# Attention in pairs of row groups: one value bank, narrower side windows and three copies a unit

## The chip, the cores and the metric

One core of a Trainium2 chip runs the whole program. The metric is the device time of one execution in microseconds; lower is better. TensorE (PE) does matrix products and transposes, VectorE (DVE) and ScalarE (ACT) elementwise work, GpSimd (POOL) some adds and a few DMAs, and SyncE's queue (SP) issues nearly all DMAs.

## What is computed

A backbone of two layers over 1024 latent tokens (a grid of 16 rows and 64 columns) and 256 context tokens, width 1024, float32. Each layer normalises and modulates, projects into three groups (a bidirectional mLSTM, a neighbourhood attention, a gated linear recurrence), projects the joined results back and adds an MLP. The change lies in the attention alone. Cut to what matters of it:

```python
for each latent query (row r, column c), 8 heads of 64 channels:
    keys  = 8 rows x 16 columns of the grid around it, and all 256 context tokens
    s     = q . k / 8 (+ relative-position bias on the grid keys)
    o     = softmax(s) @ v
context queries (first layer only): softmax(q . k_ctx / 8) @ v_ctx
```

## The kernel before

Two heads go together (`hp`, 0 to 3); `e` is the head in the pair. `na_prep` loads q and k of two heads, normalises them, transposes them and splits them into two float32r parts (`KH`, `KL`, and `QS` with both parts of q one above the other), so that a score is the sum of two products. `na_att(hp, ...)` is then the attention of these two heads. It runs for 4 pairs of heads in 2 layers.

A unit is one query tile of 128 queries for both heads. In the first layer the context gives two units (256 queries). The latents give eight: four column tiles `b` of 16 query columns, each with two row groups `g` of 8 query rows. A latent unit does, in this order:
- scores (L795, L799): keys of 12 grid rows (11 for `g` = 0) by 32 columns beginning at column 0, 8, 24 or 32, so 384 or 352 columns of one PSUM bank a head, and 256 context keys of both heads in a third bank. Each is two products (`KH`, `KL`). They take all three banks of tag "a".
- softmax: for each head VectorE adds the table (bias and masks, `tab`, 32 columns a key row) and takes the minimum of the negated scores (L809), then the same over the context keys (L813); ScalarE's exponential (L816) writes `S` and the sums `den`.
- `side()`: steps of other work, which are the preparation of the next two heads and half of the output projection (L1325, evacuated by VectorE at L1342 to the residual in DRAM).
- `softmax_pv`: ten transposes of `S` on TensorE (L688), five key tiles for each head: four tiles of head 0 into one bank, four of head 1 into another, the last context tile of both into a third (tags "b", "b", "q", which take turns and are also used by `na_prep`). They are copied into `PT`: head 0's by ScalarE (L705), head 1's by VectorE (L707), the third bank by ScalarE (L690). In row group 0 the third key tile has 96 keys only, so its two banks need three copies each, since tiles of one height go together.
- the sums: a reciprocal of `den` (L710), a copy that spreads it over 64 channels a head (L712, `rb`), and its transpose (L714) into the one bank of tag "c".
- the value products (L718) into the same bank, 64 channels of either head side by side: values `VB` of the grid (four tiles of 4 rows x 32 columns, loaded by four DMAs at L778, three buffers) and `VC` of the context.
- the exit (L826, L827; L755, L756 for the context): ScalarE copies the result into `yr`, VectorE multiplies it by the transposed reciprocals, which it reads in the bank.

A planner of the framework orders the instructions of each engine when the program is built: it takes, of those that it thinks ready by its own durations, the one that was traced first, and adds all semaphore waits. So an engine's order can differ from the traced one, but once built it is fixed, and a waiting instruction holds all behind it. A tile's buffer comes free when its last reader is done. `bank(tag)` gives a PSUM bank; the numbers of banks are p 1, q 1, a 3, b 2, c 1.

## Time and profile before

| | |
|---|---|
| median of 3 runs | 3128.67 us (3122.56 to 3129.33) |
| span of the profiled execution | 3122.6 us |
| TensorE busy | 3016.5 us (97%) |
| VectorE busy | 1898.7 us (61%) |
| ScalarE busy | 1129.1 us (36%) |
| first attention stretch | 528 to 735 us |
| second attention stretch | 2140 to 2348 us |

Busy time is the time in which an engine had at least one instruction under way. Matmuls overlap in the engine, so a row's duration is longer than what the instruction holds the engine for; the distance between two starts tells that. The granted clock (PEclk) is a share of full speed.

### The profile page before, as it was taken

Reading aid. Unit: us, or ns where it says so; the run is one execution under the profiler, and the core shown is the slowest. Engines: PE = TensorE matmul, PEld = TensorE weight load, DVE = VectorE, ACT = ScalarE, POOL = GpSimd, SP = SyncE. Lnnn points to the kernel's source line nnn. Section 1 sums busy time; section 2 is a strip of 40 time slices with the busy share of each in tenths; the row PEclk is TensorE's granted clock in tenths of the full one; section 3 lists DMA queues with packets and bytes.
Section 4 is the critical chain, followed back from the end, with each engine's and each line's share of the span. In section 5 each row is a group of like instructions: output and inputs, shape, how many; then the busy total and the mean of one; then the engine's idle time right before and its main releaser. Section 6 shows DMA issues by size and latency. Waiting matters only on the chain.

```text
span 3122.6 us, 47473 instructions
## 1 busy us (share of the span) xinstructions
PE 3016.5 (97%) x18250; PEld 2553.0 (82%) x18250; DVE 1898.7 (61%) x4318; ACT 1129.1 (36%) x2011; POOL 288.9 (9%) x252
## 2 busy tenths in 40 slices
PE   7999998999899999999999999998899999999999
PEld 6888887878788888887778889997787777887877
DVE  5757654887887666455444584755787444444444
ACT  4632223674422222233222453234564223332222
POOL 0410010122200000010000511002222000000000
PEclk9999999999899999999999999999999999999999
DMA  9624667865233444233333532348753332343333
GB/s 272 223 73 124 174 172 206 234 186 176 67 109 109 123 127 124 79 108 99 92 94 95 176 122 82 101 123 222 223 169 113 95 95 88 99 117 90 93 96 93
DMA packets 531098, 410.73 MB, mean 132 GB/s; under 512 B 27580, under 2 KB 496536, under 8 KB 530872
## 3 DMA queue, kind: packets, MB, share of 16 engines
q1 hardware_dynamic: 519448, 387.41, 42.1%
q0 software_dynamic: 8576, 15.00, 1.5%
q10 hardware_dynamic: 2848, 5.28, 0.6%
q8 instruction: 144, 2.36, 0.3%
q14 instruction: 82, 0.67, 0.1%
HBM read 339.72 MB, written 67.53 MB: 130 GB/s over the span
## 4 chain that ended last, share of the span: by engine, by line
PE 70%; DVE 11%; DMA 10%; issue 2%; ACT 2%; SPq 1%; POOL 0%; ACTq 0%; DVEq 0%; POOLq 0%
PE psa L436 15%; PE psa L1477 14%; PE psq L436 5%; PE psp L436 5%; PE psp L1477 5%; PE psq L1477 5%; PE psp L451 4%; DMA mr<-in_w_mod_dram 4%; PE psq L451 4%; PE psp L1325 2%; DVE ma L312 2%; PE psc L718 2%; DVE wl L201 1%; PE psa L1325 1%; PE psb L688 1%
## 5 line engine op out<-in xcount | busy, mean ns | idle before, releaser
L200 ACT ACTIVATE wh<-wr 128x1024 fp32r<-128x1024 f32 (+3 forms) x356 | 361.6, 1021 | 946.5 <-PE psa L1477 307.3
L201 DVE TENSOR_TENSOR wl<-wr,wh 128x1024 fp32r<-128x1024 f32 (+3 forms) x356 | 425.0, 1198 | 386.4 <-ACT wh L200 380.0
L436 PE MATMUL psa<-xlo,wh 128*128 128x512 f32 (+1 forms) x856 | 319.7, 374 | 2.2 <-DVE xlo L412 2.2
L436 PE MATMUL psa<-xh,wh 128*128 128x512 f32 (+1 forms) x856 | 319.4, 373 | 2.4 <-ACT xh L411 2.3
L436 PE MATMUL psa<-xh,wl 128*128 128x512 f32 (+1 forms) x856 | 319.6, 373 | 1.4 <-DVE wl L201 1.4
L1477 PE MATMUL psa<-hl,wh 128*128 128x512 f32 (+1 forms) x768 | 286.0, 373 | 0.6 <-DVE hl L211 0.6
L1477 PE MATMUL psa<-hh,wh 128*128 128x512 f32 (+1 forms) x768 | 284.2, 375 | 0.3 <-ACT wh L200 0.3
L1477 PE MATMUL psa<-hh,wl 128*128 128x512 f32 (+1 forms) x768 | 277.9, 373 | 0.6 <-DVE wl L201 0.6
L1481 DVE SCALAR_TENSOR_TENSOR res<-psa,modt,res 128x512 f32<-128x512 f32 (+1 forms) x192 | 131.0, 693 | 170.3 <-PE psa L1477 169.9
L436 PEld LDWEIGHTS psa<-xh,wh 128*128 128x128 f32 x856 | 162.1, 190 | 33.4 <-ACT xh L411 3.1
L436 PEld LDWEIGHTS psa<-xlo,wh 128*128 128x128 f32 x856 | 162.1, 189 | 33.1 <-DVE xlo L412 2.6
L436 PEld LDWEIGHTS psa<-xh,wl 128*128 128x128 f32 x856 | 162.1, 189 | 32.3 <-DVE wl L201 2.2
L377 POOL TENSOR_TENSOR acc<-acc,nsq 128x512 f32<-128x512 f32 (+1 forms) x56 | 77.9, 1401 | 1026.9 <-ACT nsq L376 976.5
L1477 PEld LDWEIGHTS psa<-hh,wh 128*128 128x128 f32 x768 | 144.3, 188 | 34.6 <-ACT wh L200 8.6
L451 PE MATMUL psp<-wl,xh 128*128 128x256 f32 (+1 forms) x560 | 164.0, 293 | 4.3 <-DVE wl L201 4.2
L1477 PEld LDWEIGHTS psa<-hh,wl 128*128 128x128 f32 x768 | 144.3, 188 | 28.7 <-DVE wl L201 1.5
L1477 PEld LDWEIGHTS psa<-hl,wh 128*128 128x128 f32 x768 | 144.4, 188 | 27.4 <-DVE hl L211 0.8
L210 ACT ACTIVATE hh<-rl 128x512 fp32r<-128x512 f32 (+1 forms) x160 | 93.5, 589 | 202.1 <-DVE rl L1453 202.0
L451 PE MATMUL psp<-wh,xh 128*128 128x256 f32 (+1 forms) x560 | 161.9, 289 | 2.4 <-ACT wh L200 2.4
L451 PE MATMUL psq<-wh,xh 128*128 128x256 f32 (+1 forms) x560 | 161.7, 289 | 1.4 <-ACT usq L605 0.9
L451 PE MATMUL psq<-wl,xh 128*128 128x256 f32 (+1 forms) x560 | 160.6, 287 | 0.0
L451 PE MATMUL psp<-wh,xlo 128*128 128x256 f32 (+1 forms) x560 | 159.9, 286 | 0.0
(409 smaller groups left out, 7328.5 us busy)
## 6 DMA issues: line engine op xcount, KB each, us to landing
wr<-in_w_mlp_dram SPq DMA_DIRECT2D x256, 512.0 KB
mr<-in_w_mod_dram SPq DMA_DIRECT2D x92, 512.0 KB
wr<-in_w_in_dram SPq DMA_DIRECT2D x48, 512.0 KB
tab<-T_d SPq DMA_DIRECT2D x48, 384.0 KB
T_d<-E_d POOLq DMA_DIRECT2D x48, 256.0 KB, 6.6
ab<-row_d SPq DMA_DIRECT2D x36, 256.0 KB
xT_d<-res SPq DMA_DIRECT2D x4, 2048.0 KB
wr<-in_w_out_dram SPq DMA_DIRECT2D x32, 256.0 KB
```

What stands on the lines that cost most here:

```text
L200: act.activation(hi[:, a:b], raw[:, a:b], AF.Copy)
L201: dve.tensor_sub(lo[:, a:b], raw[:, a:b], hi[:, a:b].bitcast(F32))
L210: act.activation(hi, src32, AF.Copy)
L312: dve.scalar_tensor_tensor(a, raw[:, k], s[:, k], a, op0=OP.mult, op1=OP.add)
L377: pool.tensor_add(acc[bi], acc[bi], sq[:, :n])
L436: m = pe.matmul(t[:, :n], w[a][:, k, :], X[bi][b][:, k, :], start=(i == 0), stop=(i == 23))
L451: pe.matmul(t[:, :cols], X[bi][b][:, half * 4 + k, o:o + P], ws[half][a][:, k, :], start=(i == 0), stop=(i == 23))
L688: pe.transpose(t[:w, j * P:(j + 1) * P], S[e][:, o:o + w], permT)
L718: pe.matmul(to[64 * e:64 * e + 64, :P], vals[i][:w, 64 * e:64 * e + 64], PT[:w, e, i], start=(i == 0), stop=(i == nt - 1))
L1325: pe.matmul(t[:, :n], w[a][:, k, cc * P:(cc + 1) * P], Y[bi][b][:, k], start=(i == 0), stop=(i == 11))
L1477: m = pe.matmul(t[:, :n], w[a][:, k, cc * P:(cc + 1) * P], H[bi, k][b], start=(i == 0), stop=(i == 3 * GH - 1))
L1481: dve.scalar_tensor_tensor(xr[bi][:, ct], t[:, :n], G2[:, ct, v:v + 1], xr[bi][:, ct], op0=OP.mult, op1=OP.add)
```

## The change

`softmax_pv` is split. `transposed` does the ten transposes and their copies: with the new layout all grid tiles of a unit have one height `w`, and three banks with four, two and four tiles get one copy each (VectorE, ScalarE, ScalarE). `pv` does the sums and the value products of both units of a pair, with the products in the first half of one bank "c" and the transposed reciprocals in the second, and one exit for 256 queries. The reciprocal is taken of the spread sums directly. A pair is the two row groups of a column tile, or the two context tiles. The outer column tiles (`b` = 0 and 3) take 24 key columns (from 0 and from 40), the inner ones 32; every unit takes 12 key rows. `PT` has three buffers instead of two, `VB` two instead of three. The rest of the difference removes comments and is left out here.

```diff
-        def softmax_pv(npl, S, den, tiles, vals, permT, ydst):
-            PT = npl.tile([P, 2, 5, P], F32, name=nm("PT"), tag="PT", bufs=2)
-            nt = len(tiles)
-            if nt == 2:
-                groups = [[(0, 0), (0, 1), (1, 0), (1, 1)]]
-            else:
-                groups = [[(0, i) for i in range(4)], [(1, i) for i in range(4)], [(0, 4), (1, 4)]]
-            for gi, gr in enumerate(groups):
+        def transposed(npl, S, w, permT):
+            PT = npl.tile([P, 10, P], F32, name=nm("PT"), tag="PT", bufs=3)
+            tl = [(e, i * w, w) for e in range(2) for i in range(3)] if w else []
+            tl += [(e, 3 * w + i * P, P) for e in range(2) for i in range(2)]
+            o = 10 - len(tl)
+            for a, b, q in ((0, 4, dve), (4, 6, act), (6, 10, act)):
+                if a < o:
+                    continue
                 t = bank("bbq")
-                for j, (e, i) in enumerate(gr):
-                    o, w = tiles[i]
-                    pe.transpose(t[:w, j * P:(j + 1) * P], S[e][:, o:o + w], permT)
-                if len(gr) == 2:
-                    act.activation(PT[:, :, 4], t[:, 0:2 * P].rearrange("p (k q) -> p k q", q=P), AF.Copy)
-                    continue
-                if nt == 2:
-                    act.activation(PT[:, :, 0:2], t.rearrange("p (e k q) -> p e k q", e=2, q=P), AF.Copy)
-                    continue
-                e = gi
-                j = 0
-                while j < 4:
-                    j2 = j
-                    w = tiles[j][1]
-                    while j2 < 4 and tiles[j2][1] == w:
-                        j2 += 1
-                    src = t[:w, j * P:j2 * P].rearrange("p (k q) -> p k q", q=P)
-                    if e == 0:
-                        act.activation(PT[:w, e, j:j2], src, AF.Copy)
-                    else:
-                        dve.tensor_copy(PT[:w, e, j:j2], src)
-                    j = j2
-            dve.reciprocal(den, den)
-            rb_ = npl.tile([P, 2, 64], F32, name=nm("rb"), tag="rb", bufs=2)
-            dve.tensor_copy(rb_, den.unsqueeze(2).to_broadcast([P, 2, 64]))
+                h = tl[a - o][2]
+                for j in range(a, b):
+                    e, c, _ = tl[j - o]
+                    pe.transpose(t[:h, (j - a) * P:(j - a + 1) * P], S[e][:, c:c + h], permT)
+                src = t[:h, 0:(b - a) * P].rearrange("p (k q) -> p k q", q=P)
+                if q is dve:
+                    dve.tensor_copy(PT[:h, a:b], src)
+                else:
+                    act.activation(PT[:h, a:b], src, AF.Copy)
+            return PT
+        def pv(npl, units, permT, ydst):
             to = bank("c")
-            pe.transpose(to[:, P:2 * P], rb_.rearrange("p e d -> p (e d)"), permT)
-            for i in range(nt):
-                w = tiles[i][1]
-                for e in range(2):
-                    pe.matmul(to[64 * e:64 * e + 64, :P], vals[i][:w, 64 * e:64 * e + 64], PT[:w, e, i],
-                              start=(i == 0), stop=(i == nt - 1))
-            ydst(to[:, :P], to[:, P:2 * P])
+            for u, (PT, den, loc, w, vc) in enumerate(units):
+                rb_ = npl.tile([P, 2, 64], F32, name=nm("rb"), tag="rb", bufs=2)
+                dve.reciprocal(rb_, den.unsqueeze(2).to_broadcast([P, 2, 64]))
+                pe.transpose(to[:, (2 + u) * P:(3 + u) * P], rb_.rearrange("p e d -> p (e d)"), permT)
+            for u, (PT, den, loc, w, vc) in enumerate(units):
+                n = len(loc) + 2
+                for i in range(n):
+                    for e in range(2):
+                        es = slice(64 * e, 64 * e + 64)
+                        if i < len(loc):
+                            v, p_ = loc[i][:w, es], PT[:w, 3 * e + i]
+                        else:
+                            c = i - len(loc)
+                            v, p_ = vc[:, c, es], PT[:, 6 + 2 * e + c]
+                        pe.matmul(to[es, u * P:(u + 1) * P], v, p_, start=(i == 0), stop=(i == n - 1))
+            ydst(to[:, 0:2 * P], to[:, 2 * P:4 * P])
 
         anchors = []
 
         def new_den():
             return sm.tile([P, 2], F32, name=nm("den"), tag="den", bufs=4)
         def na_att(hp, npl, stacks, yr, side):
             QS, KH, KL = stacks
             VC = npl.tile([P, 2, P], F32, name=nm("VC"), tag="VC", bufs=1)
             uv = u_nv[l]
             sp.dma_start(VC, uv[0:NCTX, hp * P:(hp + 1) * P].rearrange("(t p) c -> p t c", p=P))
             if not last:
+                units = []
                 for qt in range(2):
                     tS = bank("a")
                     S = []
...
                         dve.tensor_scalar(nmx, mx, -1.0, None, op0=OP.mult)
                         act.activation(s_[:, :256], sv, AF.Exp, bias=nmx, accum_out=den[:, e:e + 1])
                         S.append(s_)
-                    def yd(t, r, qt=qt):
-                        act.activation(yr[:, qt * P:(qt + 1) * P], t, AF.Copy)
-                        dve.tensor_mul(yr[:, qt * P:(qt + 1) * P], yr[:, qt * P:(qt + 1) * P], r)
                     side()
                     phase(f"na_att{l}")
-                    softmax_pv(npl, S, den, [(0, P), (P, P)], [VC[:, 0], VC[:, 1]], ident, yd)
+                    units.append((transposed(npl, S, 0, ident), den, [], 0, VC))
+                def yd(t, r):
+                    act.activation(yr[:, 0:2 * P], t, AF.Copy)
+                    dve.tensor_mul(yr[:, 0:2 * P], yr[:, 0:2 * P], r)
+                pv(npl, units, ident, yd)
             for ct, bs in enumerate(((0,), (1, 2), (3,))):
                 tab = []
                 for e in range(2):
...
                     pool.tensor_add(tv, tv, crm[ct].rearrange("p (r c) -> p r c", c=32))
                     tab.append(tb_)
                 for b in bs:
-                    VB = npl.tile([P, 4, P], F32, name=nm("VB"), tag="VB", bufs=3)
-                    c0 = (0, 8, 24, 32)[b]
+                    cw = (24, 32, 32, 24)[b]
+                    kc = (0, 8, 24, 40)[b]
+                    to = 8 if b == 3 else 0
+                    w = 4 * cw
+                    nl = 3 * w
+                    VB = npl.tile([P, 4, P], F32, name=nm("VB"), tag="VB", bufs=2)
                     for r in range(4):
-                        sp.dma_start(VB[r * 32:(r + 1) * 32],
+                        sp.dma_start(VB[r * cw:(r + 1) * cw],
                                      bass.AP(tensor=uv.tensor,
-                                             offset=uv.offset + (NCTX + r * 64 + c0) * 512 + hp * P,
-                                             ap=[[512, 32], [4 * 64 * 512, 4], [1, P]]))
+                                             offset=uv.offset + (NCTX + r * 64 + kc) * 512 + hp * P,
+                                             ap=[[512, cw], [4 * 64 * 512, 4], [1, P]]))
+                    units = []
                     for g in range(2):
-                        nr = 11 if g == 0 else 12
-                        nl = nr * 32
-                        r0 = 0 if g == 0 else 4
-                        kc = (0, 8, 24, 32)[b]
+                        r0 = 4 * g
                         qo = NCTX + (1 - g) * 512 + (3 - b) * P
                         tC = bank("a")
                         tL = []
...
                             tl = bank("a")
                             tL.append(tl)
                             for i, K_ in enumerate((KH, KL)):
-                                kv = K_[e][:, NCTX:].rearrange("p (r c) -> p r c", c=64)[:, r0:r0 + nr, kc:kc + 32]
-                                pe.matmul(tl[:, :nl].rearrange("p (r c) -> p r c", c=32), QS[e][:, qo:qo + P], kv,
+                                kv = K_[e][:, NCTX:].rearrange("p (r c) -> p r c", c=64)[:, r0:r0 + 12, kc:kc + cw]
+                                pe.matmul(tl[:, :nl].rearrange("p (r c) -> p r c", c=cw), QS[e][:, qo:qo + P], kv,
                                           start=(i == 0), stop=(i == 1))
                         for e in range(2):
                             for i, K_ in enumerate((KH, KL)):
...
                         S = []
                         den = new_den()
                         for e in range(2):
                             s_ = npl.tile([P, 640], F32, name=nm("S"), tag="S", bufs=4)
                             m1_ = sm.tile([P, 1], F32, name=nm("m1"), tag="m1", bufs=4)
                             m2_ = sm.tile([P, 1], F32, name=nm("m2"), tag="m2", bufs=4)
-                            dve.tensor_tensor_reduce(out=s_[:, 0:nl], in0=tL[e][:, :nl],
-                                                     in1=tab[e][:, 1 - g, 0:nl],
-                                                     scale=-1.0, scalar=3.0e38, op0=OP.add, op1=OP.min,
+                            tv = tab[e][:, 1 - g].rearrange("p (r c) -> p r c", c=32)[:, :, to:to + cw]
+                            dve.tensor_tensor_reduce(out=s_[:, 0:nl].rearrange("p (r c) -> p r c", c=cw),
+                                                     in0=tL[e][:, :nl].rearrange("p (r c) -> p r c", c=cw),
+                                                     in1=tv, scale=-1.0, scalar=3.0e38, op0=OP.add, op1=OP.min,
                                                      accum_out=m1_)
                             dve.tensor_tensor_reduce(out=s_[:, nl:nl + 256], in0=tC[:, e * 256:(e + 1) * 256],
                                                      in1=zcol.to_broadcast([P, 256]), scale=-1.0, scalar=m1_,
...
                             act.activation(s_[:, :nl + 256], s_[:, :nl + 256], AF.Exp, bias=m2_, scale=-1.0,
                                            accum_out=den[:, e:e + 1])
                             S.append(s_)
-                        tiles = [(i * P, min(P, nl - i * P)) for i in range(3)] + [(nl, P), (nl + P, P)]
-                        vals = [VB[:, i + g] for i in range(3)] + [VC[:, 0], VC[:, 1]]
-                        def yd(t, r, b=b, g=g):
-                            cs = slice(16 * b, 16 * b + 16)
-                            tv = t.rearrange("p (r c) -> p r c", r=8)
-                            dst = yr[:, NCTX:].rearrange("p (r c) -> p r c", c=64)[:, 8 * g:8 * g + 8, cs]
-                            act.activation(dst, tv, AF.Copy)
-                            dve.tensor_mul(dst, dst, r.rearrange("p (r c) -> p r c", r=8))
                         side()
                         phase(f"na_att{l}")
-                        softmax_pv(npl, S, den, tiles, vals, flip, yd)
+                        units.append((transposed(npl, S, w, flip), den, [VB[:, i + g] for i in range(3)], w, VC))
+                    def yd(t, r, b=b):
+                        dst = yr[:, NCTX:].rearrange("p (r c) -> p r c", c=64)[:, :, 16 * b:16 * b + 16]
+                        act.activation(dst, t.rearrange("p (r c) -> p r c", r=16), AF.Copy)
+                        dve.tensor_mul(dst, dst, r.rearrange("p (r c) -> p r c", r=16))
+                    pv(npl, units, flip, yd)
```

## Rows read from the trace of the kernel before

**Rows 1.** page, busy us of each engine (share of the span) and instructions
```profile
PE 3016.5 (97%) x18250; PEld 2553.0 (82%) x18250; DVE 1898.7 (61%) x4318; ACT 1129.1 (36%) x2011; POOL 288.9 (9%) x252
```

**Rows 2.** windows: stretch, length, busy us by engine, granted clock, DMA
```profile
528.00:735.00 207.00, 196.41 (x1603) 166.82 (x1604) 166.73 (x551) 132.54 (x344) 43.31 (x24) 0.98 0.69 197
630.00:680.00 50.00, 46.38 (x410) 38.83 (x408) 44.63 (x152) 37.54 (x98) 11.67 (x6) 0.97 0.69 192
2140.00:2348.00 208.00, 191.75 (x1521) 157.58 (x1520) 157.38 (x498) 121.80 (x307) 47.21 (x25) 0.97 0.75 213
```

**Rows 3.** waits of PE, 528 to 735 us: total, times, longest
```profile
PE psc L714 <- DVE yr L827: 2.4, 3, 1.1
PE psb L688 <- ACT S L816: 0.9, 1, 0.9
```

**Rows 4.** waits of PE, 2140 to 2348 us
```profile
PE psa L795 <- DVE m L809: 3.9, 4, 2.3
PE psa L799 <- DVE m L813: 3.1, 3, 2.3
```

**Rows 5.** timeline of PE, score products: start, us, what
```profile
646.35 0.28 PE L741 MATMUL psa<-KL,QS 128*128 128x256 f32 x1
646.47 0.33 PE L795 MATMUL psa<-KH,QS 128*128 128x352 f32 x1
646.63 0.33 PE L795 MATMUL psa<-KL,QS 128*128 128x352 f32 x1
...
653.71 0.34 PE L795 MATMUL psa<-KL,QS 128*128 128x384 f32 x1
653.89 0.28 PE L799 MATMUL psa<-KH,QS 128*128 128x256 f32 x1
```

**Rows 6.** timeline of PE, value products of one unit
```profile
640.42 0.27 PE L688 MATMUL psb<-idj,S 128*128 128x128 f32 x1
640.53 0.27 PE L714 MATMUL psc<-idj,rb 128*128 128x128 f32 x1
640.74 0.88 PE L718 MATMUL psc<-PT,VB 128*64 128x128 f32 x12
641.44 0.61 PE L718 MATMUL psc<-PT,VC 128*64 128x128 f32 x8
641.98 0.66 PE L688 MATMUL psb<-idj,S 128*128 128x128 f32 x4
```

**Rows 7.** line L714, what ended its engine's idle time: us, times
```profile
  DVE yr L827: 6.7, 10
  DVE rb L712: 2.5, 1
```

**Rows 8.** lines by shape, DVE, 528:735: count, busy us, mean ns, idle
```profile
L809 DVE CUSTOM_DVE_ANT_0 S<-psa,tab 128x384 f32<-128x384 f32 x32 | 17.1, 550 | 2.8 <-PE psa L795 2.7
L809 DVE CUSTOM_DVE_ANT_0 S<-psa,tab 128x352 f32<-128x352 f32 x32 | 16.0, 515 | 0.9 <-PE psb L688 0.5 <-issue 0.4
L827 DVE TENSOR_TENSOR yr<-yr,psc 128x128 f32<-128x128 f32 x28 | 7.8, 278 | 0.8 <-ACT yr L826 0.7
L707 DVE COPY PT<-psb 128x512 f32<-128x512 f32 x11 | 7.6, 688 | 2.4 <-PE psb L688 1.7 <-PE psc L718 0.7
L707 DVE COPY PT<-psb 128x256 f32<-128x256 f32 x11 | 4.6, 422 | 2.1 <-PE psc L718 2.1
```

**Rows 9.** lines by shape, DVE, whole span
```profile
L712 DVE COPY rb<-den 128x128 f32<-128x128 f32 x72 | 26.3, 365 | 4.8 <-PE psc L714 3.3
L710 DVE RECIPROCAL den<-den 128x2 f32<-128x2 f32 x72 | 11.4, 159 | 9.0 <-ACT S L816 7.2 <-ACT S L751 1.5
L1248 DVE RECIPROCAL rc<-dn 128x4 f32<-128x4 f32 x36 | 6.2, 175 | 0.7
L1247 DVE TENSOR_TENSOR dn<-dn,tmg 128x4 f32<-128x4 f32 x36 | 5.8, 162 | 0.8
```

**Rows 10.** waits of the SP queue, 528 to 735 us
```profile
SPq L778 <- PE psc L718: 5.9, 8, 1.4
```

## The prediction, made before the changed kernel was run

> **What bounds the kernel now.** I read the page first: TensorE is busy for 97% of the span, VectorE for 61% [rows 1]. The edit touches only the attention, so I looked for the two stretches in which its lines run and cut them out: 528 to 735 us in the first layer, 2140 to 2348 us in the second [rows 2]. There TensorE is busy for 196.4 of 207 and 191.8 of 208 us, VectorE for 166.7 and 157.4, ScalarE for 132.5 and 121.8. So TensorE is the bound with some 27 us of open gaps, and VectorE is the next one. A look inside the first stretch shows how near: in 630 to 680 us VectorE is busy for 44.6 of 50 us, and TensorE misses 3.6. The granted clock was 0.98 and 0.97 over the two stretches, so short spells at the lower level cost some 4 and 6 us there [rows 2].
>
> Then the waits: in the first layer TensorE's longest named wait is the transpose of the reciprocal sums (L714), which waits for the product into yr (L827) to leave the single bank "c"; in the second it is the scores, waiting for VectorE to read the three "a" banks [rows 3, 4]. Both point to VectorE as the one that TensorE waits for. The span (3122.6 us) is that of the lowest of the three runs (3122.56), so nothing to speak of lies around it; I work in differences and set them against the median, 3128.67.
>
> **The change, part by part.** There are 72 units (a unit: one query tile of two heads): 64 of latents, 8 of context in the first layer; in pairs, 36.
>
> Score columns. TensorE's price is not the duration of a row but the distance from one start to the next: 0.16 us for 352 columns, 0.18 for 384, 0.12 for 256 [rows 5]. That is (0.18 - 0.12) / 128 = 0.47 ns a column, and 0.135 us for the new 288. A side tile has four such products in either row group: 4 x (0.16 - 0.135) + 4 x (0.18 - 0.135) = 0.28 us less. A middle tile goes from 352 to 384 in one group: 4 x 0.02 = 0.08 more. There are 16 pairs of each: 16 x (0.08 - 0.28) = **-3.2 us** on TensorE, in work that nothing hides, since TensorE is the bound.
>
> Value products. They are 64 columns wide, two side by side. Going in costs something: the transpose of the sums takes 0.21 us to the next start where a transpose among its like takes 0.11. Going out too: twelve products take 0.70 us, so eight should take 0.47, and the last eight take 0.54 [rows 6]. That is 0.10 + 0.07 a unit. If both units' products stand together, 36 of 72 such passages go: 36 x 0.17 = **-6.1 us**. Bounds: -6.1, or 0 if the planner lets the first unit's products go ahead alone.
>
> One bank and one exit a pair. TensorE waited ten times for yr at L714, 6.7 us counted on its weight loads [rows 7]. The bank changes hands half as often and with another unit's work between; I take **-2 us**, with 0 and -6.7 as bounds, since part of a wait that goes is taken over by the next one.
>
> Three copies a unit. ScalarE and VectorE do the copies, and neither is the bound. For the first row group VectorE's copies of 256, 128 and 128 columns (0.42, and twice 0.28, as its product of that size) become one of 512, 0.69 [rows 8]: 0.29 x 32 units = 9.3 us less VectorE work. But the first bank now holds three tiles of the first head and one of the second, so its copy can't start before the second head's exponential; before, it needed the first head's alone. In the first stretch TensorE's transposes waited 0.9 us in all for exponentials [rows 3]; a share like that again gives **+1 us**; bounds 0 and ten times that.
>
> Side tables and exit on VectorE. The table sum took 0.550 us for 384 columns and 0.515 for 352 [rows 8], 1.1 ns a column. Side tiles save 64 and 96 columns in each of two heads, 16 pairs: 5.6 us; middle tiles give back 1.1. Two yr products of 0.278 us [rows 8] become one of 256 columns, about 0.42 as the copy of that size: 0.14 x 36 = 5 us.
>
> Reciprocals. Before: a reciprocal of two elements (0.159 us) and a copy that spreads it over 128 (0.365 on average). Now: one reciprocal over all 128 [rows 9]. No row shows one of that size. From below, a VectorE operation of 128 columns takes 0.28 us [rows 8]. From above: the reciprocals of 2 and of 4 elements take 159 and 175 ns, while a plain product of 4 elements takes 162 [rows 9]. So two more elements cost 16 ns, 8 ns each, and 128 would take 0.159 + 126 x 0.008 = 1.17 us. I take the upper end, because its rows are of the same operation. That is 1.17 - 0.52 = 0.65 us more a unit, 72 x 0.65 = 47 us. [...]
>
> So VectorE gains 47 - 9.3 - 4.5 - 5 = 28 us of work over both stretches: 324 becomes 352 of 415 us, 85%. It is not the bound on average. What is exposed is the latency before L714: its matmul needs the reciprocal of the second unit, and behind the waiting transpose stand the next pair's scores on TensorE. Of 72 such transposes 11 found VectorE late [rows 7], a share of 0.15. With 0.65 us more in each of 36 pairs, 36 x 0.65 x 0.15 = **+3.5 us**. Bounds: below nothing, -2, if the reciprocal is as short as the lower price, and 36 x 1.3 = +47 if both reciprocals of every pair are waited for.
>
> Buffers. The value tile VB has two buffers instead of three, and each of its four loads, which stand in SP's one queue, waits for the products two tiles back; behind them stand weights, tables and the rows of the side work. With three buffers the queue waited 5.9 us for this in the first stretch, never over 1.4 at once [rows 10], and VB is not among TensorE's long waits [rows 3, 4]. A pair takes some 10 us (207 us for 20 pairs, [rows 2]), and the load can start that far ahead of its use, so I take 0; if SP falls behind it costs what it waited before, some 6 us.
>
> Sum: -3.2 - 6.1 - 2 + 1 + 3.5 = **-6.8 us**: 3121.9 us.
>
> **The rivals.**
> *VectorE takes the wait over (slower).* The bank and the mode changes are saved, but each pair's products wait for the second reciprocal, because the planner places them by its own idea of its length: +0.65 x 36 = +23 instead of +3.5. With the rest of the sum (-10.3) that is +13: 3142. It decides from 10.3 / 36 = 0.29 us a pair on. For it: the two stretches where VectorE stands at 80% and more, and the upper price of the reciprocal. Against: in most units L714 found VectorE done [rows 7]. Were both reciprocals waited for, +37: 3165. [...]
>
> *The savings don't come as described.* The first unit's products go ahead on their own, as soon as its copies are there, so the passages stay at 72; then -3.2 - 2 + 1 + 3.5 = -0.7: 3128. For it: the work is queued by what is ready, and the first unit is ready early. Against: both units' sums are transposed into the shared bank ahead of any product, which may hold the first back.
>
> *The reciprocal is quick (0.28 us).* Then VectorE loses 72 x 0.24 + 19 = 36 us of its 324; the exposed term turns from +3.5 to about -2 and the waits of the second layer's scores, 7.0 us [rows 4], fall by half: -3.2 - 6.1 - 2 + 1 - 2 - 3.5 = -15.8: 3113.
>
> **How the numbers follow.** About 0.2% (6 us) is what a measurement of this kernel can tell from no change. Forecast: 0.40, a spread of 3116 to 3127 around 3122 (the spells of lower clock, 4 to 6 us a stretch, may come or go with the gaps); six tenths of it, 0.24, lie below the line at 3122.4, 0.16 within it. Rival one 0.25: 0.22 over 3134.9, 0.03 within. Rival two 0.21: 0.17 within, 0.02 on either side. Rival three 0.14, all faster. Together: faster 0.24 + 0.02 + 0.14 = 0.40, same 0.36, slower 0.24. The range leaves out 0.08 below and 0.12 above: 3107 to 3147. The likeliest case's own range is 3116 to 3127.
>
> **What would show it.** In the trace of the changed kernel: score products of 288 columns starting 0.13 to 0.14 us apart; 36 passages into the value products, each with forty in a row (a product is issued as two; twenty if rival two holds, and sixteen in a context pair); the duration of the 128-column reciprocal (0.28 or above 0.9); VectorE busy some 180 us of the first stretch if the reciprocal is slow; and waits of TensorE at the transposed sums for the reciprocal: some 4 us in all by the forecast, over 10 by rival one. The two stretches should be some 3 to 4 us shorter each, the rest unchanged. Wrong it would be if the second stretch alone changes, if SP's waits for VB exceed 20 us with TensorE waiting behind them, or if the stages ahead of or after the attention change by more than 3 us, which no term here explains.

## The result, and the profile after

The changed kernel took **3162.89 us** (median of 4 runs, 3162.17 to 3163.38), the kernel before 3129.0 beside it: ratio **1.0105**, 95% interval 1.0087 to 1.0124. It is slower by 33 us, and the time lies above the predicted range (3107 to 3147). The page of its profile:

```profile
span 3161.1 us, 47193 instructions
PE 3036.8 (96%) x18250; PEld 2563.0 (81%) x18250; DVE 1923.2 (61%) x4146; ACT 1121.2 (35%) x1911; POOL 288.4 (9%) x252
```

Against [rows 1], TensorE has the same number of instructions and is busy 20 us longer; VectorE is busy 25 us longer.

To see where, I cut each trace at points that bound the same TensorE work: from the first score of a layer's attention to the first product of the MLP's second matrix. These are windows of four kernels, one row a layer, with the columns of [rows 2]. First the kernel before:

```profile
528.20:853.10 324.90, 305.26 (x2213) 258.00 (x2214) 261.00 (x745) 184.26 (x437) 72.82 (x45) 0.96 0.58 171
2146.30:2412.00 265.70, 249.39 (x1775) 202.74 (x1775) 208.59 (x579) 153.27 (x351) 64.08 (x36) 0.98 0.64 183
```

The changed kernel:

```profile
536.80:877.10 340.30, 309.57 (x2212) 256.11 (x2213) 275.38 (x654) 180.27 (x386) 72.42 (x44) 0.95 0.56 161
2167.90:2449.10 281.20, 256.72 (x1774) 208.11 (x1775) 221.53 (x500) 150.85 (x305) 63.34 (x36) 0.96 0.59 171
```

The changed kernel with one more edit, the context's value products traced ahead of the grid's (label e18_change_context_first below):

```profile
528.80:856.60 327.80, 303.48 (x2213) 253.25 (x2214) 272.42 (x652) 178.31 (x385) 69.42 (x44) 0.97 0.57 168
2153.90:2421.80 267.90, 247.12 (x1774) 204.21 (x1775) 217.53 (x499) 149.66 (x304) 61.95 (x36) 0.97 0.61 180
```

And the best of the mended ones, with banks by head and the narrow reciprocal besides (e16_pairs_mended):

```profile
531.40:853.90 322.50, 298.88 (x2212) 251.58 (x2213) 258.30 (x691) 181.41 (x384) 71.22 (x45) 0.98 0.59 170
2151.90:2411.90 260.00, 243.20 (x1774) 199.70 (x1775) 200.06 (x531) 153.71 (x304) 62.15 (x36) 0.99 0.64 185
```

The two windows together take 590.6 us before and 621.5 after: 15.4 more in one layer, 15.5 in the other, nearly the whole loss of 33 (the two profiled spans lie 38.5 apart). TensorE is busy 554.7 and 566.3 us in them, so its idle time rises from 36 to 55 us (+19) and its busy time by 12. The granted clock can account for most of the latter, by an estimate from these rounded clocks: 1 - 0.96 and 1 - 0.98 of the windows were a shortfall of some 18 us, 1 - 0.95 and 1 - 0.96 are some 28. In the changed kernel's timeline four transposes of `S` (L690) take 0.60 us at a granted 1.00 (from 572.03 us) and 1.12 at 0.50 (from 688.61). (In this one profile the attention also begins 8.6 us later, and stages outside the attention that move by over 3 us were one of my signs of being wrong. Nothing of the change lies ahead of it, and over the other kernels' profiles it begins anywhere from 527 to 535 us, so I put that down to the execution.)

The added idle time is mostly VectorE's. Summed over TensorE's wait lists of the two windows, its matmuls waited for VectorE for 23.2 us before, 40.8 in the changed kernel and 34.9 in e18.

What the change was to do to the value products did not happen. In the records of TensorE in order of start, counted over the whole trace (a product is issued as two: of a unit's ten, the six of the grid stand as 12 and the four of the context as 8 [rows 6]):

```
                      passages into value products   lengths of the runs of products (count)
before                81                             20 (55), 16 (7), 8 (9), others 10
after                 94                             20 (29), 8 (22), 6 (16), 12 (9), 16 (5), 40 (3), others 10
after, context first  76                             20 (53), 8 (8), 12 (5), 16 (3), others 7
```

Seen in the timeline of TensorE in the changed kernel (start us, length, line, what, count): first the 288-column scores, then one pair's products from 569.20 on.

```profile
555.80 0.29 PE L798 MATMUL psa<-KL,QS 128*128 128x288 f32 x1
555.93 0.30 PE L798 MATMUL psa<-KH,QS 128*128 128x288 f32 x1
556.07 0.30 PE L798 MATMUL psa<-KL,QS 128*128 128x288 f32 x1
...
569.20 0.88 PE L716 MATMUL psc<-PT,VB 96*64 96x128 f32 x12
569.91 0.61 PE L716 MATMUL psc<-PT,VC 128*64 128x128 f32 x8
570.35 0.83 PE L716 MATMUL psc<-PT,VB 96*64 96x128 f32 x12
571.11 0.66 PE L653 MATMUL psb<-idj,ut 128*128 128x128 f32 x4
571.60 0.60 PE L690 MATMUL psq<-idj,S 128*128 128x128 f32 x4
572.03 0.60 PE L690 MATMUL psb<-idj,S 128*128 128x128 f32 x4
...
574.83 0.66 PE L716 MATMUL psc<-PT,VC 128*64 128x128 f32 x8
```

The second unit's twelve grid products run, and its eight context products only 3.7 us later, after transposes, scores and other work. All four context tiles of a unit now lie in the last bank, which is transposed and copied last, and they are traced last. So there is a point at which the grid's products are ready and the context's are not, and, as I read it, the planner parts them there; its own durations are not on record. The scores are as forecast, 0.13 to 0.14 us apart.

### The profile page after: what moved, and what is told of

The parts are those of the page before. It is cut to its first block, busy times and chain, and to the rows that moved or that the text cites. A ratio compares the mean times of both kernels' runs of the same rounds, so it can differ in the third digit from the quotient of the medians.

```text
span 3161.1 us, 47193 instructions
## 1 busy us (share of the span) xinstructions
PE 3036.8 (96%) x18250; PEld 2563.0 (81%) x18250; DVE 1923.2 (61%) x4146; ACT 1121.2 (35%) x1911; POOL 288.4 (9%) x252
## 4 chain that ended last, share of the span: by engine, by line
PE 68%; DMA 12%; DVE 11%; issue 2%; ACT 2%; SPq 1%; POOL 0%; ACTq 0%; DVEq 0%; POOLq 0%
PE psa L436 14%; PE psa L1479 13%; PE psq L436 5%; DMA mr<-in_w_mod_dram 5%; PE psp L436 5%; PE psp L1479 5%; PE psq L1479 4%; PE psp L451 4%; PE psq L451 4%; DVE ma L312 2%; PE psp L1327 2%; PE psc L716 2%; PE psb L690 1%; DMA ut<-u_nq 1%; DVE wl L201 1%
```

## The experiments

Differences between kernels are taken of their ratios to the kernel before that ran beside them, at 3.1 us per 0.1%. The interval of one ratio is some 3 to 6 us either way, so that of a difference is some 4 to 8. The executions of the kernel before themselves spread over 13 to 17 us. I read nothing into differences under 3 us. Each profile shows one execution only.

### Which part costs? The reciprocal

e2_wide_recip is the kernel before with the wide reciprocal alone; e1_spread_copy the changed kernel without it.

```diff
-            dve.reciprocal(den, den)
             rb_ = npl.tile([P, 2, 64], F32, name=nm("rb"), tag="rb", bufs=2)
-            dve.tensor_copy(rb_, den.unsqueeze(2).to_broadcast([P, 2, 64]))
+            dve.reciprocal(rb_, den.unsqueeze(2).to_broadcast([P, 2, 64]))
```

> The kernel before with the wide reciprocal alone (one instruction over 128 columns in place of a reciprocal of two and a copy). Theory R: slower by most of what the change lost, 3148 to 3170. Theory P: 72 x 0.42 us more on VectorE are mostly hidden, 3128 to 3140.

> The changed kernel with one step undone: the reciprocal is again of the two sums, and a copy spreads it; pairs, narrow side tiles and three copies stay. Theory R (the wide reciprocal, 0.95 us on VectorE, is what costs): the other terms of the prediction are left, about -10 us, so 3115 to 3128 us. Theory P (the pairing costs: the products of a pair wait for its second unit, and what the planner puts around them): it stays slow, 3145 to 3160.

e2: 3142.48 us, **1.0031** [1.0017, 1.0045], some 10 us slower, between its two ranges. e1: 3152.16, **1.0058** [1.0041, 1.0075]: taking the wide reciprocal out gives back some 15 of the 33. Its duration in the changed kernel, with the two table sums and the exit (lines by shape, VectorE, whole span):

```profile
L704 DVE RECIPROCAL rb<-den 128x128 f32<-128x128 f32 x72 | 68.2, 947 | 14.1 <-ACT S L820 11.8 <-ACT S L749 2.0
L813 DVE CUSTOM_DVE_ANT_0 S<-psa,tab 128x384 f32<-128x384 f32 x64 | 33.5, 546 | 5.0 <-PE psa L798 4.4 <-PE psb L690 0.4
L813 DVE CUSTOM_DVE_ANT_1 S<-psa,tab 128x288 f32<-128x288 f32 x64 | 27.2, 445 | 1.9 <-PE psa L798 1.2 <-issue 0.4
L831 DVE TENSOR_TENSOR yr<-yr,psc 128x256 f32<-128x256 f32 x32 | 13.0, 407 | 5.8 <-ACT yr L830 5.7
```

What TensorE waited for at the transposed sums, whole span (us, times, longest). A transpose has a weight load (PEld) and a matmul (PE), each with its own idle time; the view of [rows 7] adds the two. Its 6.7 us in ten for `yr` are 4.3 us of weight loads, here, and 2.4 of matmuls [rows 3]:

```profile
PEld psc L714 <- DVE yr L827: 4.3, 7, 1.3
```

The changed kernel, then e2, then e1:

```profile
PEld psc L705 <- DVE rb L704: 7.5, 8, 3.1
PE psc L705 <- DVE rb L704: 5.6, 6, 2.9
```

```profile
PEld psc L713 <- DVE rb L711: 5.4, 2, 4.2
PE psc L713 <- DVE rb L711: 4.9, 2, 4.0
```

```profile
PEld psc L706 <- DVE rb L705: 12.1, 8, 4.1
PE psc L706 <- DVE rb L705: 10.1, 7, 3.9
```

In the kernel before one weight load waited for `rb`, 2.5 us [rows 7], and no matmul. In e2 the matmuls' wait of 4.9 us is at most half of what that kernel lost. But e1, with the narrow reciprocal, waits longer for `rb` than the changed kernel does and is 15 us faster. So this wait does not tell the reciprocal's price: it tells how late VectorE comes to it.

### Which part costs? Windows, buffers, banks, pairs

e5_windows is the kernel before with the 24-column windows alone (12 key rows everywhere, tiles of 96 keys at the sides); e9_buffers_alone and e12_vb_two have the two lines of buffers, or VB's alone; e10_pairs_alone has the pairs, with the buffers that they need, on the old windows, banks and reciprocal. e3_copy_single and e4_wide_single are the changed kernel with one unit to a bank and an exit, e3 with the narrow reciprocal besides.

```diff
-                    c0 = (0, 8, 24, 32)[b]
+                    cw = (24, 32, 32, 24)[b]
+                    kc = (0, 8, 24, 40)[b]
...
```

The buffers, both lines in e9, the second in e12:

```diff
-            PT = npl.tile([P, 2, 5, P], F32, name=nm("PT"), tag="PT", bufs=2)
+            PT = npl.tile([P, 2, 5, P], F32, name=nm("PT"), tag="PT", bufs=3)
-                    VB = npl.tile([P, 4, P], F32, name=nm("VB"), tag="VB", bufs=3)
+                    VB = npl.tile([P, 4, P], F32, name=nm("VB"), tag="VB", bufs=2)
```

The units in e3 and e4, against the changed kernel:

```diff
-                        units.append((transposed(npl, S, w, flip), den, [VB[:, i + g] for i in range(3)], w, VC))
...
-                    pv(npl, units, flip, yd)
+                        pv(npl, [(transposed(npl, S, w, flip), den, [VB[:, i + g] for i in range(3)], w, VC)], flip, yd)
```

> The kernel before with the score windows of the change alone (12 rows, 24 columns at the sides, so one tile height a unit); banks by head as before, each head's three tiles and its first context tile in one bank, units alone, narrow reciprocal, buffers as before. Theory W (the narrow windows themselves cost, by the strided table and keys): 3140 to 3155. Theory G (the new banks cost, in which the first copy waits for both heads) and theory B (the buffers cost): a little faster than before, 3120 to 3130, by 3 us of score columns and less VectorE work.

> The kernel before with the buffers of the change alone (VB two, PT three). Theory B (the loads of VB, later by one buffer, hold SP's queue): 3137 to 3145. Otherwise 3130 to 3135, no change.

> The kernel before with two VB buffers instead of three and nothing else. If the loads of VB, later by a buffer, are what the buffers of the change cost: 3136 to 3142, as with both buffer counts changed. If PT or the planner's other order is: 3130 to 3135.

> The kernel before with pairs alone (products and sums of both row groups in one bank after the second unit, one exit; windows, copies and the narrow reciprocal as before; PT three, VB two). Theory P: 3140 to 3155, with no fewer passages into the products than before. As predicted for this part: 3120 to 3130, with some 45 passages.

> The changed kernel with both undone, the wide reciprocal and the pairing: every unit has its own bank for the products, its own exit and the narrow reciprocal; narrow side tiles and three copies stay. Theory R: 3115 to 3130, no better than with the pairs kept. Theory P: 3115 to 3130, and 20 us or more faster than with the pairs kept.

> The changed kernel with the pairing alone undone; the wide reciprocal, narrow side tiles and three copies stay. Theory R: it stays slow, 3150 to 3170. Theory P: most of the loss is gone, 3125 to 3140.

e5: 3133.75, **1.0000** [0.9990, 1.0010]. e9: 3139.03, **1.0015** [1.0001, 1.0029]; e12: 3139.99, **1.0019** [1.0009, 1.0030], so some 6 us for VB's third buffer on this kernel. e10: 3157.23, **1.0069** [1.0055, 1.0083]: 22 us, of which the buffers are 5. e3: 3148.73, **1.0051** [1.0032, 1.0071]; e4: 3148.12, **1.0049** [1.0031, 1.0068]. Of these e9, e12 and e10 came as one of their theories had it (e10 2 us above its range); e5 and e4 fell between their two ranges, and e3 lies some 19 us above what either theory allowed.

So pairs cost some 17 us on the kernel before (e10 less e9) and 17 with the wide reciprocal (the change less e4), but 2 with the narrow one (e1 less e3). The wide reciprocal costs 10 on the kernel before and 15 with pairs, but nothing in the changed kernel with single units (e4 less e3). **The parts don't add.**

e10 also shows that the planner parts units with the old banks, in which only the last context tile lies apart: 93 passages, with 18 and 2 products fifteen times each where 20 stood before. Its two windows:

```profile
533.20:874.90 341.70, 312.08 (x2213) 261.09 (x2214) 264.92 (x725) 183.85 (x417) 71.45 (x45) 0.96 0.56 162
2171.10:2445.30 274.20, 254.95 (x1774) 208.11 (x1775) 211.27 (x564) 153.62 (x336) 61.43 (x36) 0.98 0.62 177
```

How VB's price comes about is open. SP's queue waits longer for the value products in e12, but it does so in e5 too, which has three buffers and loses nothing. Whole span, in before, the changed kernel, e12 and e5 (us, times, longest):

```profile
SPq L778 <- PE psc L718: 17.8, 14, 5.4
```

```profile
SPq L782 <- PE psc L716: 25.4, 16, 5.0
```

```profile
SPq L778 <- PE psc L718: 26.0, 22, 5.7
```

```profile
SPq L782 <- PE psc L718: 26.0, 18, 5.3
```

### The banks

The changed kernel's first bank mixes three tiles of the first head with one of the second. e7_banks_by_head is e3 with one bank a head; e6_buffers and e8_head_banks_old_buffers are e3 and e7 with the old numbers of buffers.

```diff
-            for a, b, q in ((0, 4, dve), (4, 6, act), (6, 10, act)):
+            for a, b, q in ((0, 3, act), (3, 6, dve), (6, 10, act)):
```

> The changed kernel without wide reciprocal and without pairs (e3_copy_single), and with the buffers of before: VB three, PT two. Theory B: back to 3120 to 3132. Theories G and W: no change, 3140 to 3152.

> The same as e3_copy_single, with three copies a unit still but banks of three, three and four tiles: first head's grid tiles (ScalarE), second head's (VectorE), all context tiles (ScalarE). The first bank needs the first head's exponential alone. Theory G: back to 3118 to 3132. Theories B and W: no change, 3140 to 3152.

> e7_banks_by_head with the buffers of before (VB three, PT two): narrow windows, three copies in banks of 3, 3 and 4 tiles, units alone, narrow reciprocal. If the buffers and the banks each cost about half of the 8 to 16 us that e3_copy_single lost: 3128 to 3135, level with the kernel before. If what costs is that all four context tiles come in the last bank with the longest copy (so that grid and context products part): still 3138 to 3146, and some 90 passages into the products.

e6: 3141.24, **1.0023** [1.0014, 1.0032]. e7: 3141.32, **1.0026** [1.0015, 1.0037]. e8: 3131.93, **0.9990** [0.9980, 1.0001]. Against e3, banks by head give back 8 us and the buffers 9, each with intervals that still meet, and both e6 and e7 lie in the range that their text gave to "no change"; together they give back 19, clear of the intervals, and the kernel of single units is level with before. So three copies a unit are no loss in themselves; the mixed set of banks is, by some 10 us (e6 to e8).

That the first bank waits for both heads was my reading, and the traces do not bear it out. In e3 and e7 TensorE's transposes (L690, matmuls, whole span) waited about as long for exponentials (1.4 us each). What differs is the wait for VectorE to clear a bank at L667 (`ql`), in e3

```profile
PE psq L690 <- DVE ql L667: 8.0, 3, 4.6
PE psb L690 <- DVE ql L667: 1.3, 2, 1.1
```

and in e7

```profile
PE psb L690 <- DVE ql L667: 1.2, 2, 0.9
```

(e7 waits 2.0 us at L662 besides, where e3 waits none.) The edit also moves the first copy from VectorE to ScalarE and makes VectorE's copies shorter (384 columns for 512: 0.55 us in e16 below, which has e7's banks, where e3 took 0.68); no run parts these.

### The order of the value products

Three kernels with the context's products traced ahead of the grid's, nothing else: e11_context_first from e1, e13_best_single from e8, e18_change_context_first from the changed kernel itself.

```diff
-                for i in range(n):
+                nl_ = len(loc)
+                order = list(range(nl_, n)) + list(range(nl_))
+                for i in order:
...
-                        pe.matmul(to[es, u * P:(u + 1) * P], v, p_, start=(i == 0), stop=(i == n - 1))
+                        pe.matmul(to[es, u * P:(u + 1) * P], v, p_, start=(i == order[0]), stop=(i == order[-1]))
```

> e1_spread_copy (the change with the narrow reciprocal) with the products of the context traced before those of the grid, so that a unit's products start when its last copy is there and stand together. If the many passages cost what the prediction put on them, 0.17 us each, some 30 fewer of them give 5 us: 3144 to 3150. If TensorE then waits for the last copy instead: 3150 to 3165.

> e8_head_banks_old_buffers with context products first: units alone, narrow windows, banks by head, narrow reciprocal, buffers of before. Some 70 passages into the products instead of 92, at 0.17 us each 4 us less: 3124 to 3130, faster than the kernel before. If TensorE waits for the last copy instead: 3132 to 3140.

> The changed kernel as it is, with one step changed: the context products are traced before the grid products. If the parted products cost in the changed kernel what they cost with the narrow reciprocal (12.5 us): 3146 to 3154, some 70 passages instead of 94. If the wide reciprocal hides that: 3158 to 3165.

e11: 3139.61, **1.0018** [1.0008, 1.0027], some 12 us less than e1; e11 and e18 both came out below the ranges of their texts. e18: 3136.74, **1.0011** [1.0001, 1.0021]: this edit alone gives back **some 29 of the 33 us**, with the wide reciprocal, the buffers and the mixed bank in place. The rows of e18 above say where: in the two windows TensorE's idle time falls from 55 to 45 us and its busy time from 566 to 551, some 10 of these 16 by the clock (0.95 and 0.96 become 0.97). The wait of the matmuls for `rb` at the transposed sums falls from 5.6 us to 2.3. With this order the wide reciprocal costs nothing either: e18 has it and e11 has not, and their ratios are 1.0011 and 1.0018. Two rows of its TensorE timeline show a unit whole:

```profile
565.89 0.66 PE L718 MATMUL psc<-PT,VC 128*64 128x128 f32 x8
566.38 0.83 PE L718 MATMUL psc<-PT,VB 96*64 96x128 f32 x12
```

e13: 3134.78, **1.0007** [0.9995, 1.0020], no gain on e8, though its passages fall from 92 to 72. That speaks against passages as the price: the 18 that e18 has fewer than the changed kernel are 18 x 0.17 = 3 us by the rows of before, a tenth of its gain.

### Can the pairs pay?

e16_pairs_mended is e11 with banks by head (pairs, narrow windows, narrow reciprocal, context first). e17_singles_mended is e16 with one unit to a bank, as in e3. e19_mended_wide is e16 with the wide reciprocal. e20_spread_act has e16's spread copy on ScalarE:

```diff
-                dve.tensor_copy(rb_, den.unsqueeze(2).to_broadcast([P, 2, 64]))
+                act.activation(rb_, den.unsqueeze(2).to_broadcast([P, 2, 64]), AF.Copy)
```

> The change with three steps mended: narrow reciprocal, banks by head, context products first; pairs and its buffers (VB two, PT three) stay. If pairs cost by themselves: 3138 to 3155, over 8 us above the same with units alone (e17). If pairs cost only because a unit's products part: 3130 to 3138.

> e16_pairs_mended with units alone and the same buffers (VB two, PT three): 3130 to 3138, and 5 to 10 us above e13 if the buffers cost.

> e16_pairs_mended with the wide reciprocal. If its cost is its time on VectorE and adds to whatever else is there: +8 to +12, 3141 to 3146. If it costs only by waits at the sums that the other faults make long: 3132 to 3137.

> e16_pairs_mended with the spread copy on ScalarE, so that VectorE loses 72 copies of 0.365 us (one took 1.77) and ScalarE, at 60% in these stretches, takes 72 of some 0.27. If VectorE is what still holds the attention: 3122 to 3130. If the floor is TensorE's order and its gaps: 3130 to 3136.

e16: 3132.70, **0.9995** [0.9984, 1.0005]. By its rows above the windows take 8 us less than before and TensorE is busy 12 us less in them. That is not the terms for TensorE coming true: by the same estimate some 9 of the 12 are the clock (0.98 and 0.99 where it was 0.96 and 0.98), in one execution that lies some 8 us below the median of e16, and the medians are level. e17: 3133.70, **0.9999** [0.9988, 1.0010]; it has two VB buffers where e13 has three (and three of PT for two) and is no slower, so here the buffers of the change cost nothing. e19: 3142.04, **1.0021** [1.0008, 1.0033]: the reciprocal has a price again, 8 us over e16. e20: 3132.72, **0.9997** [0.9985, 1.0008]: with the least VectorE work in the windows of all kernels (432.9 us by its row of sums, 469.6 in the kernel before) nothing more is gained. Mended, the pairs cost nothing and bring nothing that this measurement can tell. No version beat the kernel before.

## Why the prediction was wrong

**The step that failed** is the one on the value products: "if both units' products stand together, 36 of 72 such passages go", -6.1 us. I let the planner choose between forty in a row and twenty in a row. It had a third choice, to part a unit, and the change offers it: I had read that the first bank now waits for both heads, but not that the last bank now holds all the context and is read last. Pairs alone offer it too (e10). The passages rose from 81 (not 72, since some units were parted before too) to 94. Tracing the context first brings them to 76 and the time back to some 3 us over before. By my own price, 0.17 us each, 13 more of them are only 2 us. Rival two ("the savings don't come as described") had the place right, but foresaw only that the saving would be missing, not a loss.

That the passage itself is not the price follows from e13. What e18 shows is that the order cost idle time and clock, about 10 us each, the clock's by the estimate above. Here is a piece of the changed kernel in which both stand together (windows, columns as above):

```profile
660.00:670.00 10.00, 9.46 (x92) 7.79 (x91) 7.19 (x22) 6.67 (x22) 3.59 (x2) 1.00 0.44 133
670.00:678.60 8.60, 6.35 (x47) 4.08 (x45) 8.33 (x23) 6.36 (x15) 0.00 (x0) 1.00 0.95 261
678.60:692.20 13.60, 8.69 (x50) 6.53 (x51) 6.70 (x18) 3.77 (x8) 3.60 (x2) 0.63 0.68 119
692.20:700.00 7.80, 7.47 (x55) 5.67 (x54) 7.45 (x23) 6.41 (x15) 0.00 (x0) 1.00 0.26 67
```

From 670 us VectorE is busy for 8.33 of 8.6 us and TensorE for only 6.35; then the granted clock falls to 0.63 over 13.6 us. In that stretch one more hole opens, here in the timelines of TensorE and of VectorE (in brackets the idle time before, and what ended it), and the load that VectorE waited for on SP's queue:

```profile
688.61 1.12 PE L690 MATMUL psb<-idj,S 128*128 128x128 f32 x4 [4.67 <-DVE ql L667]
```

```profile
687.34 0.69 DVE L645 TENSOR_TENSOR ut<-ut,rsn 128x512 f32<-128x512 f32 x1 [5.61 <-DMA ut<-u_nq]
```

```profile
677.80 0.51 SPq L642 DMA_DIRECT2D ut<-u_nq  x1
```

TensorE waits for VectorE to clear a bank for it, and VectorE waits for rows that a DMA loads for the next heads. That load was issued at 677.80, some 9.5 us before VectorE could use it, in stretches in which the DMA engines were busy at 0.95 and then 0.68. The losses are spread over such holes: no wait in TensorE's lists adds up to over 6 us in a layer. Nor does more idle time always stand with a lower clock: the windows of e10 above have 49 us of it against 36, at the clock of before (0.96 and 0.98).

So the order's share is measured (29 of 33 us), and how it costs them stays open. The same edit brings 29, 12 and no us in three settings. It changes the whole order that the planner makes, so the parted products and the rest of that order were not told apart, and I have no run that separates the order from the load of VectorE and of SP's queue.

Point by point:
- **Score columns**, -3.2: the distances are as forecast (0.13 to 0.14 us), and e5 measured 0 with 3 either way. Right on TensorE, not seen in the time.
- **One bank and one exit**, -2: I had read the 6.7 us of [rows 7] as weight loads alone; the matmuls' share was 2.4. In that view's sum the waits for `yr` fell from 6.7 us to 0.3, as said; waits for `rb` took their place (13.1 for 2.5; matmuls 5.6 for none). With the passages, pairs were to bring 8 us; they cost 17 alone (e10 less e9), and nothing once mended (e16, e17).
- **Three copies**, +1 with ten times that as the upper bound: the mixed set of banks costs some 8 us (e3 to e7) to 10 (e6 to e8). The size was at its bound, but the mechanism that I priced, a wait for the second head's exponential, is not what the traces show. The matmuls of the transposes waited 2.3 us for exponentials in the changed kernel and 1.8 before.
- **VectorE's sum**, +28 us: +27.3 in the two windows (496.9 against 469.6). The match is luck. Without the wide reciprocal (e1) the windows hold 466.2 us, so the reciprocal brought some 31 for my 47, and all the savings together some 3 for my 19, though their rows came as the terms had them: the 288-column table sum takes 445 ns and the exit 407.
- **Reciprocal**, 1.17 us taken: 0.947 measured, nearer to it than to the 0.28 of a plain operation. The cost was taken as a longer reciprocal on VectorE times the share of late transposes. That share was of another wait: of my 11 late transposes ten were entries for `yr`, weight loads and matmuls counted together, and one for `rb` [rows 7]. In the changed kernel 8 of 72 weight loads and 6 of 72 matmuls found `rb` late. The +3.5 stands against 10 us alone (e2), 15 with the pairs (the change less e1), 8 mended (e19 less e16), and nothing in two other settings (e4 less e3, e18 less e11). So the price depends on the order around it, and no share of late transposes gives it.
- **VB with two buffers**, 0, with 6 named as the price if SP falls behind: e12 took 6 us more. In the changed kernel the queue's waits are 25.4 us and TensorE waits 2.7 for VB, which was one of my signs of being wrong; but e5 shows that such queue waits need not cost, and e17 against e13 that the fewer VB buffers need not either.
- **Rival one** (VectorE takes the wait over, 3142) has the sign, and e2 and e19 stand at 3142 themselves. Its mechanism, a wait for the reciprocal in every pair, does not show: two matmuls waited for `rb` in e2, three in e19, six in the changed kernel. (Of the 80% and more that spoke for it, the second stretch had 157.4 of 208 us, 76%.) It was not the main cause either: e18 keeps the wide reciprocal and stands at 3137.

Lone prices of the parts are 10 (reciprocal), 6 (VB), 0 (windows) and 17 (pairs) on the kernel before, and some 8 for the mixed banks (e3 to e7), 41 together where the change measured 33; I had -6.8. The reciprocal, VB and the banks stood in my text with bounds of terms that I took near zero, and all five erred to the same side.

## What to carry to other kernels

Where a planner may issue part of an accumulation before the rest, look at which operands are ready last and try those first in the traced order; here that was worth 29 us of 33 in the changed kernel, 12 in another and nothing in a third. A term that comes from one view should be checked for what the view counts: the waits of weight loads and matmuls (here 4.3 and 2.4 us of one sum) are not two waits, and a wait for one thing gives no share for another. Costs measured one by one need not add: make the whole version that undoes the suspect, not only the parts.

## What the runs showed of the hardware

- A VectorE reciprocal of 128 columns took 0.947 us in the changed kernel (930 to 956 ns over 72). With 159 ns for two columns [rows 9] that is (947 - 159) / 126 = 6.25 ns a column between the two sizes, where the table sum costs (546 - 445) / 96 = 1.05.
- In the two windows the changed kernel has 19 us more of idle time on TensorE, and the lower granted clock (0.95 and 0.96, for 0.96 and 0.98) takes some 10 us besides, by the estimate above; e10 has 13 us more of idle time at the clock of before (0.96 and 0.98). In the piece shown, the 13.6 us from 678.6 us were granted 0.63 (0.50 from 678.6 to 682 and again from 686 on, 1.00 from 682 to 685), after 8.6 us at 1.00 in which TensorE had been busy for 6.35.
- Some 20 passages fewer into and out of the 64-column products (e13 against e8) gave no time, though the one unit in the timeline of the kernel before shows a longer distance at either end [rows 6]: 0.21 us after the transpose ahead of them, where a transpose among its like takes 0.11, and 0.54 for the last eight, where twelve take 0.70.
